# Full-width state sums and transpositions for the samples' heads

## The chip, the cores and the metric

The kernel runs on one core of one Trainium2 chip. The metric is the device time of one execution in microseconds (us); "the time before" is the median of three runs. The engines are TensorE (PE, with its weight loads shown apart as PEld), VectorE (DVE), ScalarE (ACT), GpSimd (POOL) and SyncE (SP), which issues most of the transfers.

## The reference

One layer of a hybrid decoder is computed for a prompt of 1024 tokens and for 8 samples of 4 tokens (32 rows, `NS`). A matrix-memory branch (mLSTM, 4 heads of 128 by 128) and a sliding-window attention run side by side on the same projected input; their outputs are gated, summed and projected. The change lies in the memory branch of the samples. There every sample brings its own state `C` per head, and the output of one head is

```
num = einsum('bhts,bhse->bhte', s, v) + w_inter * einsum('bhtd,bhde->bhte', q, C)
dot = sum(s) + w_inter * einsum('bhtd,bhd->bht', q, n)
h   = num / maximum(abs(dot), exp(-m_hat))
h   = h * rsqrt(mean(h * h) + NORM_EPS) * g_mn
```

All arithmetic is float32.

## The kernel before

The large products (input projections, output projections) are made on PE with operands split into a high and a low part, three products of 128x512 for each one of the reference; some are formed by a seven-product scheme for 2x2 blocks. This work is one long stream on PE, named `bx`, `bw`, `by`, `bz` in the middle of the kernel, `ax`, `aw`, `ay`, `az` for the attention's projection and `g_w_mo` and `foX`, `foW`, `foY`, `foZ` behind it. Its weights come by SP, ACT casts the high parts (`wh_...`) and DVE subtracts the low parts (`wl_...`).

Smaller pieces of work (attention units, memory heads, samples) are generators. A planner (`Side`) keeps an estimated clock, advanced by `mm` and `tr` with a cost per product, and lets a generator emit its next piece between two products of the stream when the delay that the generator yielded has passed and the PSUM banks that it named are free. The order of all PE instructions is fixed in the order in which they are emitted (`in_order`). In the middle of the kernel DVE and ACT are left to the framework, which orders by its own costs.

`sample_head(h)` is the generator of one head of the samples; it is run for h = 0 to 3, one at a time. Its first part makes the products of the 8 samples' queries with their states: 8 products `sn` with 32 stationary columns each, put in four strips of 32 PSUM partitions. So the 128 partitions of `ns4` (in the tile `sz`) hold four partial sums of the same 32 rows. Heads 0 and 2 only add theirs to the list `tails`. Heads 1 and 3 go on with a tail for two heads; here is what a *visit* means in this document:

- L1242 to L1246: the *state sums*. The four partial sums of a head are added on PE: the stationary operand is the piece of the constant table `cst` from column `C_S32` (745) with 32 columns, where row r has a one in column r mod 32; the moving operand is `ns4`, 128 by 129. Two such products, one for each head, go to the PSUM tile `st`, and ACT copies `st` to `sz` (32 partitions).
- L1247 to L1257: the squares, denominators and the scaling of both heads' rows, on ACT and DVE.
- L1258 to L1263: the *transpositions*. Each head's 32 by 128 rows are transposed on PE into the PSUM tile `sty`, and DVE scales each result by `gmn` into `gs`. In the code a transposition is followed by its scaling, then the second transposition and its scaling.

There are two such tails in the kernel, each with one visit for the state sums and one for the transpositions. `gs` is read some products later by the gate of the same head (`head_gate.samples`).

The column table continues behind `C_S32` (32 columns) with `C_BM` (8 columns, ones that tell which sample a row belongs to) and `C_S64` (64 columns, another summing pattern) and ends at `C_END` = 849: 104 columns in all.

In the profile every matmul has the line of the helper `mm` (L271), every transposition that of `tr` (L276) and the work of DVE and ACT in this part that of `call` (L220), so that groups are told apart by tile. A float32 matmul shows as two instructions of each kind, a transposition as one.

Of the kernel before, what the change touches and what calls it, by code (L numbers as in the profile page):

```python
# [15 lines left out]
ALU = mybir.AluOpType  # L16
# [8 lines left out]
NS = NB * NT  # L25
# [11 lines left out]
C_ID, C_S9, C_TRI, C_CM, C_AM, C_TS, C_CS, C_RS, C_S32, C_BM, C_S64 = 0, 128, 137, 265, 393, 649, 681, 713, 745, 777, 785  # L37
C_END = 849
# [135 lines left out]
def body(tc, a):  # L174
    nc = tc.nc
    with ExitStack() as ctx:
# [11 lines left out]
        def pb(shape, name):  # L188
            return ps.tile(shape, F32, tag="b", bufs=2, name=name)

        def po(shape, name):
            return ps.tile(shape, F32, tag="o", bufs=2, name=name)

        def ht(shape, name, dt=F32):
            return sp.tile(shape, dt, tag="half", bufs=50, name=name)

        def sm(shape, name, bufs=3, dt=F32):
            return sp.tile(shape, dt, tag=name, bufs=bufs, name=name)
# [8 lines left out]
        def in_order(ins, eng="PE"):  # L207
            i = getattr(ins, "ins", ins)
            no_sync(i, [last[eng]] if eng in last else [])
            last[eng] = i  # L210
# [27 lines left out]
        V, S, G = Ordered(nc.vector, "V"), Ordered(nc.scalar, "S"), Ordered(nc.gpsimd, "G")  # L238
# [28 lines left out]
        def mm(out, lhsT, rhs, start, stop, share=1, more=False):  # L267
            n = int(np.prod(rhs.shape[1:]))
            side.now += max(n, 250) / 2400 if rhs.dtype == F32R else max(n * 4 // share, 128) / 2400
            side.products += 1  # L270
            in_order(nc.tensor.matmul(out, lhsT, rhs, start=start, stop=stop, skip_group_check=more))  # L271

        def tr(out, in_, idn):
            side.now += 0.11
            side.products += 1
            in_order(nc.tensor.transpose(out, in_, idn))  # L276
# [43 lines left out]
        cst = cp.tile([128, C_END], F32, name="cst")  # L320
# [3 lines left out]
        ident = cst[:, C_ID:C_ID + 128]  # L324
# [4 lines left out]
        gmn, bada, gnorm = vec[:, 0:4], vec[:, 4:20], vec[:, 20:28]  # L329
# [656 lines left out]
        gs = cp.tile([128, NH, NS], F32, name="gs")  # L986
# [51 lines left out]
        def head(h):  # L1038
# [128 lines left out]
            if h == 2:  # L1167
                at["n0"], at["n1"] = (cp.tile([128, NH, NB], F32, name=n) for n in ("n0", "n1"))
                dma(at["n0"], a["state_n"])
                for i in range(NH):  # L1170
                    side.add("s", sample_head(i), "ob")
# [3 lines left out]
        def sample_head(h):  # L1175
            an, sxb, fls, wes = st["an"], st["sxb"], st["fls"], st["wes"]
            z = ht([128, 512], "sz")
# [28 lines left out]
            for b, m in zip(bs, ns_):  # L1206
                vf, vm = ht([NS, 512], f"vf{h}"), ht([96, 512], f"vm{h}", F32R)
                w = m * 129 + m % 2
# [31 lines left out]
                return  # L1240
            yield 3.0, "o"
            tot = po([128, 2, 129], f"st{h}")  # L1242
            for i, (_, n4) in enumerate(tails):
                mm(tot[:NS, i], cst[:, C_S32:C_S32 + NS], n4, start=True, stop=True)
            ns = z[:NS, 0:258].rearrange("p (m e) -> p m e", e=129)
            S.copy(ns, tot[:NS])  # L1246
            ssq = sm([NS, 2], "sssq", 2)  # L1247
            for i in range(2):
                jk = sm([128, 128], "mjk", 2, BF16)
# [6 lines left out]
            for i in range(2):  # L1256
                V.tensor_scalar(ns[:, i, 0:128], ns[:, i, 0:128], d[:, i:i + 1], r[:, i:i + 1], op0=ALU.mult, op1=ALU.mult)  # L1257
            yield 4.0, "b"  # L1258
            ty = pb([128, 2, NS], f"sty{h}")
            for i, (g, _) in enumerate(tails):  # L1260
                tr(ty[:, i], ns[:, i, 0:128], ident[:NS, :NS])
                V.tensor_scalar(gs[:, g], ty[:, i], gmn[:, g:g + 1], None, op0=ALU.mult)
                samples_done.append(g)  # L1263
            tails.clear()
            if h == NH - 1:
# [1108 lines left out]
```

## Time and profile before

| | |
|---|---|
| Median of three runs | 834.73 us (834.29 to 835.82) |
| Profiled execution, its own time | 832.12 us |
| Its span in the trace | 830.4 us |
| PE busy | 810.4 us (98%), 5129 instructions |
| PE weight loads busy | 669.3 us (81%) |
| DVE busy | 593.8 us (72%) |
| ACT busy | 420.5 us (51%) |
| POOL busy | 67.2 us (8%) |
| Granted PE clock, mean | 0.997 |

The profiled execution is 2.6 us shorter than the median of the runs, and 1.7 us longer than its own span. In the timelines each row has the start, the duration, the engine, the line, the operation, the tile written and the tiles read, and (for PE) the size of the stationary operand as rows*columns and of the result. Matmuls overlap: what a piece of work costs PE is read from the starts, not from the durations.

### The profile page before, as it was taken

To read this page: it belongs to the slowest core of one execution; us is meant where nothing else is said; L and a number is where in the kernel's file an instruction comes from. 1 tells how busy PE (TensorE), PEld (TensorE's weight loads), DVE (VectorE), ACT (ScalarE), POOL (GpSimd) and SP (SyncE) were. 2 spreads that over 40 slices of the span, in tenths; PEclk is the share of its full clock that TensorE was granted. 3 is DMA by queue.
4 is the path that set the end of the run, shared out by engine and by line. 5 is a ranking of instruction groups with operands and counts; after the bars stand their busy time and mean duration, and the time that the engine had idled before them with its cause. 6 is when DMAs were issued, how large, how long until landed. Compare 5 with 4: busy or idle time off the path is not lost. (4 is left out here: it accounts for less than half of the span.)

```text
span 830.4 us, 15038 instructions
## 1 busy us (share of the span) xinstructions
PE 810.4 (98%) x5129; PEld 669.3 (81%) x5129; DVE 593.8 (72%) x1479; ACT 420.5 (51%) x1030; POOL 67.2 (8%) x128
## 2 busy tenths in 40 slices
PE   6999999999999999999899999999999999999996
PEld 3779897888788788888788877887888789997775
DVE  4889886656656456475577785897569988974776
ACT  5664365555474564555455453544346654334343
POOL 0120000000000001000001000000002104250000
PEclk9999999999999999999999999999999999999998
DMA  9997766356436425479856345464336785643633
GB/s 334 378 357 238 184 201 213 118 150 217 143 111 189 114 85 150 140 240 286 268 188 205 120 141 155 143 203 142 103 117 196 230 288 172 212 146 122 202 109 108
DMA packets 106689, 153.96 MB, mean 185 GB/s; under 512 B 20448, under 2 KB 54368, under 8 KB 106580
## 3 DMA queue, kind: packets, MB, share of 16 engines
q1 hardware_dynamic: 100964, 142.25, 54.1%
q10 hardware_dynamic: 4176, 6.56, 2.2%
q0 software_dynamic: 1472, 4.20, 1.4%
q8 instruction: 40, 0.66, 0.3%
q14 instruction: 37, 0.30, 0.1%
HBM read 109.22 MB, written 44.75 MB: 185 GB/s over the span
## 5 line engine op out<-in xcount | busy, mean ns | idle before, releaser
L220 ACT ACTIVATE p<-p,nmx 128x256 f32<-128x256 f32 (+1 forms) x64 | 31.0, 486 | 12.4 <-DVE nmx L220 12.1
L271 PE MATMUL g_aq<-h_h,wh_aq 128*128 128x384 f32 (+1 forms) x96 | 32.2, 336 | 0.0
L271 PE MATMUL g_aq<-h_h,wl_aq 128*128 128x384 f32 (+1 forms) x96 | 30.9, 322 | 0.0
L271 PE MATMUL g_aq<-h_l,wh_aq 128*128 128x384 f32 (+1 forms) x96 | 30.8, 321 | 0.0
L271 PE MATMUL g_w_mo<-ym_l,wh_w_mo 128*128 128x384 f32 (+1 forms) x96 | 30.8, 321 | 0.0
L271 PE MATMUL g_w_mo<-ym_h,wh_w_mo 128*128 128x384 f32 (+1 forms) x96 | 30.8, 321 | 0.0
L271 PE MATMUL g_w_mo<-ym_l,wl_w_mo 128*128 128x384 f32 (+1 forms) x96 | 30.8, 321 | 0.0
L220 DVE CUSTOM_DVE_ANT_0 p<-sc,cst,sink 128x256 f32<-128x256 f32 (+1 forms) x64 | 26.2, 464 | 5.3 <-PE sc L271 5.2
L259 POOL DMA_DIRECT2D oD<-uqv x16 | 8.9, 554 | 183.2 <-ACT uqv L220 161.0
L220 DVE COPY p<-pt 128x512 f32<-128x512 f32 (+1 forms) x16 | 10.5, 657 | 13.6 <-PE pt L276 13.6
L271 PEld LDWEIGHTS g_aq<-h_h,wh_aq 128*128 128x128 f32 x96 | 18.0, 188 | 2.5 <-issue 1.5
L271 PEld LDWEIGHTS g_w_mo<-ym_l,wh_w_mo 128*128 128x128 f32 x96 | 18.0, 188 | 0.0
L271 PEld LDWEIGHTS g_aq<-h_l,wh_aq 128*128 128x128 f32 x96 | 18.1, 188 | 0.0
L271 PEld LDWEIGHTS g_w_mo<-ym_h,wh_w_mo 128*128 128x128 f32 x96 | 18.0, 188 | 0.0
L271 PE MATMUL sc<-ukv,uqv 64*128 64x256 f32 (+1 forms) x128 | 18.0, 390 | 0.0
L271 PEld LDWEIGHTS g_aq<-h_h,wl_aq 128*128 128x128 f32 x96 | 18.0, 188 | 0.0
L271 PEld LDWEIGHTS g_w_mo<-ym_l,wl_w_mo 128*128 128x128 f32 x96 | 18.0, 188 | 0.0
L220 ACT ACTIVATE p<-p,den 128x256 f32<-128x256 f32 (+1 forms) x32 | 14.5, 491 | 5.7 <-DVE den L220 5.6
L220 ACT ACTIVATE sq<-rows_h 128x512 f32<-128x512 f32 (+2 forms) x14 | 8.2, 582 | 17.8 <-issue 12.0
L220 DVE TENSOR_TENSOR et<-et,S 128x384 f32<-128x384 f32 (+1 forms) x12 | 6.1, 510 | 15.4 <-PE S L271 12.7
L271 PE MATMUL g_mq<-h_h,wh_mq 128*128 128x384 f32 (+1 forms) x48 | 16.8, 349 | 0.3 <-ACT mk L220 0.3
L276 PE MATMUL pt<-cst,p 128*128 128x128 f32 x120 | 16.4, 277 | 0.5 <-DVE mx L220 0.5
(2073 smaller groups left out, 2841.4 us busy)
## 6 DMA issues: line engine op xcount, KB each, us to landing
x<-xT SPq DMA_DIRECT2D x16, 256.0 KB, 5.6
early_h<-w_ada SPq DMA_DIRECT2D x8, 512.0 KB, 9.0
adar_ga<-w_ada SPq DMA_DIRECT2D x16, 256.0 KB, 4.0
wr_ga<-w SPq DMA_DIRECT2D x16, 256.0 KB, 2.9
wr_gm<-w SPq DMA_DIRECT2D x16, 256.0 KB, 3.6
taD<-gt SPq DMA_DIRECT2D x16, 256.0 KB, 2.2
tmD<-gt SPq DMA_DIRECT2D x16, 256.0 KB, 5.3
wor<-w_out SPq DMA_DIRECT2D x16, 256.0 KB, 5.1
```

The costliest lines, as they stand in the source:

```text
L220: ins = f(*args, **kw)
L259: ins = (eng or nc.sync).dma_start(out, in_)
L271: in_order(nc.tensor.matmul(out, lhsT, rhs, start=start, stop=stop, skip_group_check=more))
L276: in_order(nc.tensor.transpose(out, in_, idn))
```

## The change

The state sums take the stationary columns from `C_S32` to `C_END`, 104 instead of 32; their result has 104 partitions, of which the first 32 are the ones needed, and ACT's copy takes all 104. The two transpositions of a visit take all 104 partitions as input, with a 104 by 104 identity as moving operand, and their result has 128 by 104 elements for each head; the PSUM tile `sty` grows from 32 to 128 columns per head. The scaling of the squares, denominators and rows still works on the first 32 partitions. The two transpositions are emitted one behind the other, and then the two scalings, which read the first 32 columns.

```
             tot = po([128, 2, 129], f"st{h}")
+            w = C_END - C_S32
             for i, (_, n4) in enumerate(tails):
-                mm(tot[:NS, i], cst[:, C_S32:C_S32 + NS], n4, start=True, stop=True)
-            ns = z[:NS, 0:258].rearrange("p (m e) -> p m e", e=129)
-            S.copy(ns, tot[:NS])
+                mm(tot[:w, i], cst[:, C_S32:C_END], n4, start=True, stop=True)
+            nw = z[:, 0:258].rearrange("p (m e) -> p m e", e=129)
+            S.copy(nw[:w], tot[:w])
+            ns = nw[:NS]
...
             yield 4.0, "b"
-            ty = pb([128, 2, NS], f"sty{h}")
+            ty = pb([128, 2, 128], f"sty{h}")
+            for i in range(2):
+                tr(ty[:, i, 0:w], nw[:w, i, 0:128], ident[:w, :w])
             for i, (g, _) in enumerate(tails):
-                tr(ty[:, i], ns[:, i, 0:128], ident[:NS, :NS])
-                V.tensor_scalar(gs[:, g], ty[:, i], gmn[:, g:g + 1], None, op0=ALU.mult)
+                V.tensor_scalar(gs[:, g], ty[:, i, 0:NS], gmn[:, g:g + 1], None, op0=ALU.mult)
                 samples_done.append(g)
```

PE at the first state sums: the rows are products of the stream (`bw`, 128x512, from a block and a split weight), and between them the two sums.

```order
 L271 MATMUL bw<-t2l_1093,wh_pgate_6__5970 128x512
 L271 MATMUL bw<-t2h_1092,wl_pgate_6__5971 128x512
-L271 MATMUL st_6039<-sz,cst 32x129 x2
+L271 MATMUL st_6039<-sz,cst 104x129 x2
 L271 MATMUL bw<-t2h_1370,wh_pgate_6__5970 128x512
 L271 MATMUL bw<-t2l_1371,wh_pgate_6__5970 128x512
```

Their place stays; only the width of the result differs. It is the same at the second state sums (`st_6738`).

PE at the second pair of transpositions, with the semaphores for which each instruction waits (`DVE_49` counts DVE's finished instructions):

```order
 L271 MATMUL by<-t3l_1686,wh_phead_gate_7__6815 128x512
 L271 MATMUL by<-t3h_1685,wl_phead_gate_7__6816 128x512
-L276 MATMUL sty_6908<-cst,sz 128x32 [waits DVE_49] x2
+L276 MATMUL sty_6908<-cst,sz 128x104 [waits DVE_49]
+L276 MATMUL sty_6908<-cst,sz 128x104
 L271 MATMUL bx<-h_h_378,wh_phead_gate_1__6838 128x512
 L271 MATMUL bx<-h_l_379,wh_phead_gate_1__6838 128x512
```

The place is the same again. The second transposition waited for the first scaling on DVE, which reads the same PSUM tile; it now waits for nothing of its own. At the first pair (`sty_6175`) the second transposition still names DVE, but there the count is that of its own input, the rows in `sz` scaled before, and no longer that of a scaling to `gs`.

DVE at the same visit (`hg1z` and `hg` belong to the gates of a head, `wl_...` and `ws` to the weights of coming products):

```order
 L220 TENSOR_TENSOR hg1z<-p_6811,by 128x512
-L220 TENSOR_SCALAR gs<-sty_6908,vec 128x32
+L220 TENSOR_SCALAR gs<-sty_6908,vec 128x32 x2
 L220 TENSOR_TENSOR wl_phead_gate_5__6931<-ws_6883,wh_phead_gate_5__6930 128x512
 L220 TENSOR_SCALAR hg_6903<-hg_6903,hg1z 128x512
-L220 TENSOR_SCALAR gs<-sty_6908,vec 128x32
 L220 TENSOR_TENSOR ws_7072<-wr_mz_0_6979,wr_mz_1_6981 128x512
```

The second scaling moves ahead of the low part of a weight and of a gate product. Nothing else moves on any engine, SP's and POOL's queues included.

## The prediction

> **What bounds the kernel now.** First the page's busy times, then the busy time by stretches: PE is the engine to look at.
>
> ```profile
> PE 810.4 (98%) x5129; PEld 669.3 (81%) x5129; DVE 593.8 (72%) x1479; ACT 420.5 (51%) x1030; POOL 67.2 (8%) x128
> ```
>
> ```profile
> 580.00:640.00 60.00, 59.67 (x319) 49.23 (x320) 42.01 (x72) 28.16 (x54) 4.11 (x3) 1.00 0.41 122
> ...
> 760.00:800.00 40.00, 40.00 (x186) 30.32 (x185) 25.01 (x56) 17.97 (x46) 0.00 (x0) 1.00 0.36 125
> 800.00:830.40 30.40, 23.21 (x126) 19.99 (x124) 22.70 (x54) 11.14 (x32) 0.00 (x0) 0.92 0.41 143
> ```
>
> The columns are the stretch, its length, and the busy times of PE, PEld, DVE, ACT and POOL, the granted clock, the share of the DMA engines and their GB/s. PE has no idle time from 680 us to 800, and the idle time behind it is the tail after its last product. So a microsecond taken out of PE's stream ahead of that is a microsecond of the end, unless something else turns out late. Third, the list of PE's own waits from 500 us on, with the sum, the count and the longest:
>
> ```profile
> PE sty L276 <- DVE gs L220: 1.1, 2, 0.8
> PE aw L271 <- ACT aw L220: 0.2, 1, 0.2
> ```
>
> These two are all of it. The first is in the changed lines: the second transposition waits for the scaling of the first. But a busy PE need not be a PE that streams, so the fourth view is PE's timeline at the four visits, read by starts.
>
> **The state sums.** The first visit in full, and of the second the product ahead of it and the second product behind it:
>
> ```profile
> 503.05 0.39 PE L271 MATMUL bw<-t2h,wl_pgate__5971 128*128 128x512 f32 x1
> 503.37 0.63 PE L271 MATMUL st<-sz,cst 128*32 128x129 f32 x4
> 503.93 0.50 PE L271 MATMUL bw<-t2h,wh_pgate__5970 128*128 128x512 f32 x1
> 504.26 0.39 PE L271 MATMUL bw<-t2l,wh_pgate__5970 128*128 128x512 f32 x1
> ...
> 563.88 0.39 PE L271 MATMUL by<-t4h,wl_pquery_gate__6676 128*128 128x512 f32 x1
> ...
> 565.09 0.39 PE L271 MATMUL by<-t4l,wh_pquery_gate__6675 128*128 128x512 f32 x1
> ```
>
> I measure each piece from the start of the last stream product ahead of it to the start of the second one behind it, since the first one behind starts slowly (0.33 us to the next). That is 504.26 - 503.05 = 1.21 us, and 565.09 - 563.88 = 1.21. No row has 104 stationary columns. The nearest above is two float32 products of 129 columns with all 128 stationary columns, `U` of a prompt's head, also inside the stream:
>
> ```profile
> 341.80 0.39 PE L271 MATMUL bx<-h_h,wl_pgate__4064 128*128 128x512 f32 x1
> 342.03 0.61 PE L271 MATMUL U<-hv,hk 128*128 128x129 f32 x4
> 342.39 0.48 PE L271 MATMUL bw<-h_h,wh_pgate__4138 128*128 128x512 f32 x1
> 342.71 0.40 PE L271 MATMUL bw<-h_l,wh_pgate__4138 128*128 128x512 f32 x1
> ```
>
> The same four instructions cost 342.71 - 341.80 = 0.91 us. They start 0.23 us behind the product ahead, where `st` needs 0.32, and take 0.36 against 0.56. The weight loads tell why:
>
> ```profile
> 503.37 0.36 PEld L271 LDWEIGHTS st<-sz,cst 128*32 128x32 f32 x4 [0.35 <-issue]
> ```
>
> ```profile
> 341.81 0.64 PEld L271 LDWEIGHTS U<-hv,hk 128*128 128x128 f32 x4
> ```
>
> The loads of `U` begin under the stream's last product (341.80); those of `st`, with 32 columns, start only at 503.37, after 0.35 us of idle time. So a narrow stationary operand is not loaded ahead, and its width is not what it costs. I take the full-width price: 104 columns fill more than three quarters of the array, and a narrow one of three quarters in the other direction exists, `sU` with 96 rows:
>
> ```profile
> 472.80 0.40 PE L271 MATMUL by<-t4h,wl_pgate__5616 128*128 128x512 f32 x1
> 473.03 0.64 PE L271 MATMUL sU<-vm,skn 96*128 96x388 f32 x3
> 473.51 0.40 PE L271 MATMUL by<-t4h,wh_pgate__5615 128*128 128x512 f32 x1
> ```
>
> It starts 0.23 us behind the product ahead: no delay. So a visit falls from 1.21 to 0.91, 0.30 us, and two visits give **0.60 us**. The ends are no gain at all (104 treated like 32) and the strips among the rivals below.
>
> [...]
>
> ACT's copy of the sums reads 104 partitions for 32, with the same 258 elements in each:
>
> ```profile
> L220 ACT COPY sz<-st x2: 361/362/364, 504.0 to 565.4; 32x258 f32<-32x258 f32 x2
> ```
>
> ```profile
> L220 ACT COPY uqv<-oT x16: 352/373/378, 117.3 to 320.5; 128x256 f32<-128x256 f32 x16
> ```
>
> 128 partitions take 373 ns at the median where 32 take 362, so I cost it at 0.01 us twice, off PE's path, and at nothing.
>
> **The transpositions.** First visit in full; of the second the product ahead, the second transposition and the second product behind:
>
> ```profile
> 516.14 0.39 PE L271 MATMUL bw<-h_h,wl_pgate__6128 128*128 128x512 f32 x1
> 516.46 0.24 PE L276 MATMUL sty<-cst,sz 32*128 32x32 f32 x1
> 517.04 0.24 PE L276 MATMUL sty<-cst,sz 32*128 32x32 f32 x1 [0.35 <-DVE gs L220]
> 517.22 0.50 PE L271 MATMUL bw<-h_h,wh_pgate__6127 128*128 128x512 f32 x1
> 517.55 0.39 PE L271 MATMUL bw<-h_l,wh_pgate__6127 128*128 128x512 f32 x1
> ```
>
> ```profile
> 579.00 0.39 PE L271 MATMUL by<-t3h,wl_phead_gate__6816 128*128 128x512 f32 x1
> ...
> 580.33 0.24 PE L276 MATMUL sty<-cst,sz 32*128 32x32 f32 x1 [0.77 <-DVE gs L220]
> ...
> 580.85 0.40 PE L271 MATMUL bx<-h_l,wh_phead_gate__6838 128*128 128x512 f32 x1
> ```
>
> They cost 517.55 - 516.14 = 1.41 us and 580.85 - 579.00 = 1.85. For full-height transpositions in the stream there are eight of a prompt's head, `ty`:
>
> ```profile
> 444.02 0.39 PE L271 MATMUL bw<-h_h,wl_pgate__5275 128*128 128x512 f32 x1
> 444.25 1.03 PE L276 MATMUL ty<-cst,et 128*128 128x128 f32 x8
> 445.05 0.48 PE L271 MATMUL bw<-h_h,wh_pgate__5274 128*128 128x512 f32 x1
> 445.36 0.40 PE L271 MATMUL bw<-h_l,wh_pgate__5274 128*128 128x512 f32 x1
> ```
>
> Eight take 1.34 us by the same measure, 0.80 of it the eight, 0.10 each. With six fewer that is 1.34 - 0.60 = 0.74 us for two, as wide as 128 columns; 104 are no wider. The wait is gone too: nothing stands between the two transpositions, and the second one's own input was scaled before the visit. So the visits fall by 1.41 - 0.74 = 0.67 and 1.85 - 0.74 = 1.11, together **1.78 us**.
>
> What is moved on DVE: the second scaling now goes ahead of a weight's low part.
>
> ```profile
> 580.03 0.25 DVE L220 TENSOR_SCALAR gs<-sty,vec 128x32 f32<-128x32 f32 x1
> 580.19 0.68 DVE L220 TENSOR_TENSOR wl_phead_gate__6931<-ws,wh_phead_gate__6930 128x512 fp32r<-128x512 f32 x1
> ```
>
> ```profile
> 589.30 0.39 PE L271 MATMUL bz<-h_h,wl_phead_gate__6931 128*128 128x512 f32 x1
> ```
>
> That delays this low part by the 0.16 us of one scaling (580.19 - 580.03), and PE needs it nine microseconds later, so it costs nothing; if the slack were gone, 0.16. Later products that now name DVE's semaphore do so for things that the removed wait had covered; those are as old as before. DVE also waited for the second transposition behind the first scaling; that ends, and no waiting instruction stands behind it.
>
> **The sum.** 0.60 + 1.78 = 2.38 us. The profiled execution took 832.12, and would take 829.74. It lies 2.61 below the median of the runs, 834.73; the pieces are steps of PE's stream and do not depend on that difference, so against the median it is 834.73 - 2.38 = 832.35, forecast as **832.4 us**, 0.28% less. A change of 0.2%, 1.67 us, is about what a measurement of this kernel can tell from no change.
>
> **The rivals.**
>
> *The narrow treatment stays, only the wait goes.* If 104 columns or rows were loaded late as 32 are, the starts would stay slow, and only the steps between the two transpositions would shrink: from 517.04 - 516.46 = 0.58 to the 0.18 that an unhindered one takes (517.22 - 517.04), and by the second wait's row from 1.01 to 0.18, if the first of that pair stands 0.32 behind 579.00 as in the first pair. That is 0.40 + 0.83 = 1.23 us, a time of 833.5. For it: no row has 104 columns. Against it: `sU` with 96 rows is not delayed.
>
> *The gain is eaten before the attention's projection.* PE's other wait, 0.2 us at `aw`, ends a chain that runs through DVE:
>
> ```profile
> 646.46 1.11 DVE yr L220
> ```
>
> ```profile
> 627.24 0.69 DVE L220 TENSOR_TENSOR hg<-p,bw 128x512 f32<-128x512 f32 x1 [0.28 <-PE bw L271]
> ```
>
> If DVE did not get there sooner, PE would come 2.38 us earlier and wait for just as much: 834.7. For it: DVE was nearly the bound there. Against it: the work that it does then was itself released by PE's product at 627.24, so it moves along with PE.
>
> *The array takes 104 as four strips of 32.* This one makes it slower. The inner part of the state sums, 0.56 us, would then be paid four times, 3 x 0.56 x 2 visits = 3.36 us more, and each transposition four times its 0.18, 3 x 0.18 x 4 = 2.16 more, less the 1.23 of the wait: 4.29 more, 839.0. It decides from the point where the strips cost over 1.23 + 1.67 = 2.90 us. Against it: three strips of rows in `sU` run at the stream's pace, 0.16 us for a product of 388 columns (0.48 for three).
>
> **How the numbers follow.** Full gain 0.74, narrow treatment stays 0.10, eaten 0.09, strips 0.07. The best case is the full gain without the slow first product behind each piece, which `U` still shows (0.32 against 0.23): four times 0.09, so 2.74 and 832.0. The runs spread 1.5 us; half of it, 0.77, is added on both sides. Low is 832.0 - 0.77, 831.2; high is the narrow case plus as much, 833.5 + 0.77, 834.3. These hold 0.84 of the cases. Faster by over 0.2%: 0.70, the full gain less a few hundredths for the runs' scatter; within 0.2%: 0.22; slower by over 0.2%: 0.08.
>
> **What would show it.** Right: the loads of `st` begin under the product ahead, `st` starts 0.23 us behind it, and the piece measures about 0.91; the two transpositions stand 0.1 us apart, without a wait on DVE, the piece about 0.74; PE's wait at `aw` stays at some tenths, and its last product ends 2.4 us earlier. Wrong: an idle time of 0.35 ahead of the loads as before (narrow treatment), a wait of over 2 us between 640 and 650 (eaten), or pieces longer than 1.21 (strips). Transfers that land at other times, from 640 us on, could move the end without any of this.

## The result and the profile after

The changed kernel takes 831.21 us (median of five runs, 830.73 to 832.2) where the one before takes 834.73 (832.91 to 835.82 with the runs made beside it). The ratio is 0.997, with a 95% interval of 0.9955 to 0.9984: faster by 1.3 to 3.8 us. Its profiled execution took 830.97 us, with a span of 829.2. The forecast was 832.4, and the measured time lies at the lower edge of its range, so two questions remain: whether the parts do what the prediction says, and where another microsecond came from.

The page's busy times of the changed kernel, and PE's own waits from 490 us on (sum, count, longest):

```profile
PE 810.1 (98%) x5129; PEld 670.8 (81%) x5129; DVE 592.7 (71%) x1479; ACT 420.6 (51%) x1030; POOL 67.5 (8%) x128
```

```profile
PE aw L271 <- ACT aw L220: 0.2, 1, 0.2
```

The wait at `sty`, 1.1 us in two, is gone. The one at `aw` is as long as it was. PE's timeline of the changed kernel at the state sums, the first visit in full and of the second the product ahead and the second behind:

```profile
504.46 0.39 PE L271 MATMUL bw<-t2h,wl_pgate__5971 128*128 128x512 f32 x1
504.69 0.60 PE L271 MATMUL st<-sz,cst 128*104 128x129 f32 x4
505.04 0.47 PE L271 MATMUL bw<-t2h,wh_pgate__5970 128*128 128x512 f32 x1
505.36 0.39 PE L271 MATMUL bw<-t2l,wh_pgate__5970 128*128 128x512 f32 x1
...
564.22 0.39 PE L271 MATMUL by<-t4h,wl_pquery_gate__6676 128*128 128x512 f32 x1
...
565.12 0.39 PE L271 MATMUL by<-t4l,wh_pquery_gate__6675 128*128 128x512 f32 x1
```

The weight loads at the first of them:

```profile
504.46 0.61 PEld L271 LDWEIGHTS st<-sz,cst 128*104 128x104 f32 x4
```

The loads now begin at 504.46, together with the stream's last product ahead, and no idle time stands before them. `st` starts 0.23 us behind that product, and the piece is 505.36 - 504.46 = 0.90 us where it was 1.21; the second is 0.90 too. The transpositions of the changed kernel, first visit in full, of the second three rows:

```profile
517.23 0.39 PE L271 MATMUL bw<-h_h,wl_pgate__6128 128*128 128x512 f32 x1
517.46 0.34 PE L276 MATMUL sty<-cst,sz 104*128 104x104 f32 x2
517.58 0.47 PE L271 MATMUL bw<-h_h,wh_pgate__6127 128*128 128x512 f32 x1
517.89 0.39 PE L271 MATMUL bw<-h_l,wh_pgate__6127 128*128 128x512 f32 x1
...
579.02 0.39 PE L271 MATMUL by<-t3h,wl_phead_gate__6816 128*128 128x512 f32 x1
579.26 0.34 PE L276 MATMUL sty<-cst,sz 104*128 104x104 f32 x2
...
579.69 0.39 PE L271 MATMUL bx<-h_l,wh_phead_gate__6838 128*128 128x512 f32 x1
```

The two stand in one row, with no wait: 517.89 - 517.23 = 0.66 us and 579.69 - 579.02 = 0.67, where the pieces were 1.41 and 1.85. Together the four visits give 0.31 + 0.31 + 0.75 + 1.18 = 2.55 us. With PE's products of the two traces laid side by side, the changed kernel is 1.41 us late ahead of the first visit (504.46 against 503.05) and 1.16 early behind the fourth (579.69 against 580.85): 2.57 us. PE's last product, in the kernel before and then in the changed one, is 1.19 us early, so all of it reaches the end:

```profile
822.93 0.28 PE L271 MATMUL foY<-wo_p0h,u3wlD 128*128 128x256 f32 x1
```

```profile
821.74 0.28 PE L271 MATMUL foY<-wo_p0h,u3wlD 128*128 128x256 f32 x1
```

What made it late ahead of the first visit lies at 404 us, far from the change. The kernel before in two stretches of 4 us (length, busy times of PE, PEld, DVE, ACT and POOL, then the granted clock):

```profile
404.00:408.00 4.00, 1.67 (x12) 1.35 (x12) 1.65 (x4) 1.99 (x9) 0.10 (x1) 1.00 0.86 320
408.00:412.00 4.00, 4.00 (x44) 3.40 (x46) 2.46 (x5) 2.94 (x8) 0.00 (x0) 1.00 0.70 233
```

The changed kernel in the same two stretches, and what PE does there:

```profile
404.00:408.00 4.00, 1.74 (x10) 1.50 (x9) 1.38 (x3) 1.73 (x8) 0.10 (x1) 0.86 0.78 296
408.00:412.00 4.00, 4.00 (x15) 3.17 (x14) 2.32 (x4) 2.22 (x5) 0.00 (x0) 0.72 0.57 210
```

```profile
406.80 1.21 PE L271 MATMUL S<-hq,hk 128*128 128x128 f32 x4 [2.26 <-DVE C L220]
...
408.66 0.63 PE L271 MATMUL bw<-t2h,wl_pgate__4793 128*128 128x512 f32 x1
409.08 0.63 PE L271 MATMUL bx<-h_h,wh_pgate__4824 128*128 128x512 f32 x1
```

PE waits 2.26 us for DVE (2.33 in the kernel before), and then its products follow each other in 0.42 us instead of 0.23, at a granted clock of 0.72 in the mean of the stretch. In the profiled execution of the kernel before the same wait was followed by steps of 0.23 us, at a clock of 1.00. Whether such a half-speed stretch belongs to the change or to the single execution, these two profiles can't tell; the profiles of the experiments tell more of it.

### The profile page after: what moved, and what is told of

Its sections match the earlier page's. It is cut to its first block, busy times and chain, and to the rows that moved or that the text cites. A ratio compares the mean times of both kernels' runs of the same rounds, so it can differ in the third digit from the quotient of the medians.

```text
span 829.2 us, 15039 instructions
## 1 busy us (share of the span) xinstructions
PE 810.1 (98%) x5129; PEld 670.8 (81%) x5129; DVE 592.7 (71%) x1479; ACT 420.6 (51%) x1030; POOL 67.5 (8%) x128
```

## The experiments

Pieces are measured throughout as in the prediction: from the start of the last product of the stream ahead to the start of the second one behind. The theory to be tested: the width pays only where it lets the stationary operand be loaded ahead, the emitted order pays by taking PE's wait for the first scaling away, and the two add up at the end. The rivals: the gain comes from elsewhere (other executions of one of the two kernels are disturbed more), the width acts by degrees and not by a threshold, or the wait at `sty` is not due to the shared PSUM tile. Edits are shown against the changed kernel. In the table the changed kernel has five runs, each of the three parts twelve, and the kernel before 29 beside them (five beside the first row of the changed kernel).

| kernel | state sums, us | transpositions, us | median (lowest to highest), us | before, beside it | ratio, 95% interval |
|---|---|---|---|---|---|
| before | 1.21, 1.21 | 1.41, 1.85 | 834.73 | | |
| changed | 0.90, 0.90 | 0.66, 0.67 | 831.21 (830.73 to 832.2) | 834.73 | 0.9955 to 0.9984 |
| changed, again | 0.89, 0.89 | 0.67, 0.67 | 830.19 (829.96 to 831.71) | 834.29 | 0.9943 to 0.9966 |
| sums wide only | 0.89, 0.90 | 1.42, 1.84 | 833.75 (831.56 to 836.2) | 834.29 | 0.9979 to 1.0007 |
| order only | 1.22, 1.21 | 0.89, 0.89 | 832.76 (830.79 to 835.63) | 834.29 | 0.9965 to 0.9991 |
| width only | 0.90, 0.90 | 1.23, 1.73 | 833.64 (831.17 to 836.6) | 834.29 | 0.9979 to 1.0007 |

**The changed kernel again**, without an edit.

> The changed kernel once more, beside the three halves of the change on the same chip. Theory (PE's stream lost 2.57 us at the four visits and all of it reaches the end): the pieces, from the start of the last product ahead to the start of the second behind, measure 0.90, 0.90, 0.66 and 0.67 us, and the ratio to the kernel before is 0.997. Rival (part of the 3.5 us between the first medians was the change acting elsewhere): the offset of PE's products to those of the kernel before moves at other places too, at the same ones each time; the half-speed stretch of PE at 407 to 410 us, seen in the first profile of the changed kernel, comes back.

The pieces came out as expected; the time is 4.1 us less than that of the kernel before on the same chip, more than the 2.55 of the pieces. So the excess is not confined to one comparison. This profile has the half-speed stretch too: a wait of 3.2 us at `S`, and a granted clock of 0.57 from 408 to 412.

**The sums wide, the transpositions as before.**

```
             ty = pb([128, 2, 128], f"sty{h}")
-            for i in range(2):
-                tr(ty[:, i, 0:w], nw[:w, i, 0:128], ident[:w, :w])
             for i, (g, _) in enumerate(tails):
+                tr(ty[:, i, 0:NS], ns[:, i, 0:128], ident[:NS, :NS])
                 V.tensor_scalar(gs[:, g], ty[:, i, 0:NS], gmn[:, g:g + 1], None, op0=ALU.mult)
```

> Only the state sums have 104 columns; the transpositions take 32 rows and follow each other in the old order. Theory: sums 0.90 us each instead of 1.21, transpositions 1.41 and 1.85 as before, 0.62 us less in all, ratio 0.9993. Rival (the width helps only where the neighbour is wide too): sums still 1.21, ratio 1.000.

0.32 and 0.31 us by the pieces, 0.5 by the medians, and the interval holds no change. The sums alone are below what the runs can tell.

**The order alone**, with 32 columns and rows.

```
-            w = C_END - C_S32
+            w = NS
...
-                mm(tot[:w, i], cst[:, C_S32:C_END], n4, start=True, stop=True)
+                mm(tot[:w, i], cst[:, C_S32:C_S32 + w], n4, start=True, stop=True)
...
-                tr(ty[:, i, 0:w], nw[:w, i, 0:128], ident[:w, :w])
+                tr(ty[:, i, 0:NS], ns[:, i, 0:128], ident[:NS, :NS])
```

> Only the order: both transpositions ahead of both scalings, 32 columns and 32 rows as before. Theory: the wait for DVE goes (0.40 and 0.84 us), the late start and the slow first product behind stay, so the transposition pieces measure about 1.0 us each (0.32 + 0.18 + 0.18 + 0.33), sums 1.21; 1.24 us less, ratio 0.9985. Rival (the order alone does nearly everything): pieces near 0.7, ratio 0.998 or less.

PE's timeline of this kernel at the first visit:

```profile
516.32 0.39 PE L271 MATMUL bw<-h_h,wl_pgate__6128 128*128 128x512 f32 x1
516.64 0.30 PE L276 MATMUL sty<-cst,sz 32*128 32x32 f32 x2
516.87 0.50 PE L271 MATMUL bw<-h_h,wh_pgate__6127 128*128 128x512 f32 x1
517.21 0.39 PE L271 MATMUL bw<-h_l,wh_pgate__6127 128*128 128x512 f32 x1
```

0.89 us, 0.11 less than expected: the two together take 0.23 (516.87 - 516.64), where 0.18 for each was expected. The late start of 0.32 stays. The order is worth 0.52 + 0.96 = 1.48 us, the largest part of the change; by the medians it is 1.5.

**The width alone**, with a transposition followed by its scaling as before.

```
             ty = pb([128, 2, 128], f"sty{h}")
-            for i in range(2):
-                tr(ty[:, i, 0:w], nw[:w, i, 0:128], ident[:w, :w])
             for i, (g, _) in enumerate(tails):
+                tr(ty[:, i, 0:w], nw[:w, i, 0:128], ident[:w, :w])
                 V.tensor_scalar(gs[:, g], ty[:, i, 0:NS], gmn[:, g:g + 1], None, op0=ALU.mult)
```

> Only the width: sums with 104 columns, transpositions with 104 rows, but each transposition followed by its scaling. Theory: sums 0.90 each; the second transposition still waits for the first scaling, so the pieces measure about 1.25 and 1.75 us (0.1 to 0.2 less than before each); 0.9 us less in all, ratio 0.9989. Rival (the wait was only a matter of the narrow form): no wait, pieces near 0.67, ratio 0.997.

The second visit of this kernel:

```profile
580.61 0.39 PE L271 MATMUL by<-t3h,wl_phead_gate__6816 128*128 128x512 f32 x1
580.84 0.25 PE L276 MATMUL sty<-cst,sz 104*128 104x104 f32 x1
581.94 0.31 PE L276 MATMUL sty<-cst,sz 104*128 104x104 f32 x1 [0.85 <-DVE gs L220]
```

The first starts 0.23 us behind the product ahead, on time, and then the second waits 0.85 for DVE. An earlier start of the first mostly lengthens the wait: at this visit only 0.12 us of the width's 0.22 remain. So the two edits of the transpositions are worth more together (0.22 each by the width, once the wait is gone) than the width is alone.

**Other widths.** In one kernel the sums and transpositions of the first tail have 64 columns and rows and those of the second 72, in another 40 and 96.

```
-            w = C_END - C_S32
+            w = 64 if h == 1 else 72
...
-                mm(tot[:w, i], cst[:, C_S32:C_END], n4, start=True, stop=True)
+                mm(tot[:w, i], cst[:, C_S32:C_S32 + w], n4, start=True, stop=True)
```

> The changed kernel with other widths: 64 columns and rows in the tail of head 1, 72 in that of head 3. Theory (a stationary operand is loaded ahead only if it is over half of the array in both directions): head 1 as narrow as with 32, sums 1.21 us and transpositions about 1.0; head 3 as with 104, sums 0.90 and transpositions 0.66. Rival (the price falls with the width, step by step or in proportion): 64 lies between, sums near 1.1, and 72 is not yet at 0.90.

> The same with 40 in the tail of head 1 and 96 in that of head 3. Theory (over half): 40 is narrow, sums 1.21 and transpositions about 1.0; 96 is wide, 0.90 and 0.66. Rival (only full strips of 32 count, or 104 is special): 96 is narrow, or 40 costs more than 32 did because it takes two strips.

The state sums of the first of these kernels, with 64 and then with 72 stationary columns:

```profile
507.09 0.39 PE L271 MATMUL bw<-t2h,wl_pgate__5971 128*128 128x512 f32 x1
507.41 0.65 PE L271 MATMUL st<-sz,cst 128*64 128x129 f32 x4
...
508.33 0.40 PE L271 MATMUL bw<-t2l,wh_pgate__5970 128*128 128x512 f32 x1
...
567.45 0.39 PE L271 MATMUL by<-t4h,wl_pquery_gate__6676 128*128 128x512 f32 x1
567.68 0.60 PE L271 MATMUL st<-sz,cst 128*72 128x129 f32 x4
...
568.36 0.39 PE L271 MATMUL by<-t4l,wh_pquery_gate__6675 128*128 128x512 f32 x1
```

| width | state sums, us | transpositions, us |
|---|---|---|
| 40 | 1.22 | 0.90 |
| 64 | 1.24 | 0.92 |
| 72 | 0.91 | 0.64 |
| 96 | 0.91 | 0.66 |
| 104 | 0.90 | 0.66 |

Single executions took 834.18 us (64 and 72) and 834.0 (40 and 96), beside 835.92 for the kernel before; the pieces tell more. It is a threshold between 64 and 72 of 128, in columns (the sums) and in rows (the transpositions) alike, and not a price that falls with the width: 40 columns cost as much as 64, 72 as much as 104. At 64 and below the first instruction starts 0.32 us behind the stream, above it 0.23. Other small products of the kernel before show the same border. `sc` with 64 rows is late:

```profile
216.18 0.39 PE L271 MATMUL bx<-h_h,wl_phead_in__2696 128*128 128x512 f32 x1
216.50 1.14 PE L271 MATMUL sc<-ukv,uqv 64*128 64x256 f32 x8
```

All five `sc` with 64 rows and all seven `oT` with 64 columns that stand right behind a 128x512 product of the stream start 0.32 to 0.33 us behind it, and the four `sU` with 96 rows 0.23 to 0.24. What the delay is made of is not shown by any run here. What is measured is 0.09 us of late start, 0.02 on the way back (0.33 to 0.34 to the second product behind, 0.31 to 0.32 above the border), and for the four instructions of the sums another 0.2 us inside the piece.

**Two PSUM tiles.** The order of the kernel before and 32 columns, but the second transposition goes to a tile of its own.

```
-            for i in range(2):
-                tr(ty[:, i, 0:w], nw[:w, i, 0:128], ident[:w, :w])
             for i, (g, _) in enumerate(tails):
-                V.tensor_scalar(gs[:, g], ty[:, i, 0:NS], gmn[:, g:g + 1], None, op0=ALU.mult)
+                t = ty if i == 0 else pb([128, 2, 128], f"stz{h}")
+                tr(t[:, i, 0:NS], ns[:, i, 0:128], ident[:NS, :NS])
+                V.tensor_scalar(gs[:, g], t[:, i, 0:NS], gmn[:, g:g + 1], None, op0=ALU.mult)
```

The sums have 32 columns too (`w = NS`, as in the kernel with the order alone).

> The kernel before but for one thing: the second transposition of a visit writes a PSUM tile of its own instead of the other half of the first one's, with the old widths and the old order in the code. Theory (the wait comes from the shared tile, not from the order of the instructions on PE): the wait for DVE is gone although the code's order is the old one, transposition pieces about 1.0 us each, sums 1.21. Rival (PE's order of emission makes the wait): the waits of 0.35 and 0.77 us stay, pieces 1.41 and 1.85. A third possibility: the second tile's bank is not free yet, and the second transposition waits for ACT instead.

```profile
518.24 0.39 PE L271 MATMUL bw<-h_h,wl_pgate__6128 128*128 128x512 f32 x1
518.56 0.24 PE L276 MATMUL sty<-cst,sz 32*128 32x32 f32 x1
518.64 0.22 PE L276 MATMUL stz<-cst,sz 32*128 32x32 f32 x1
518.79 0.50 PE L271 MATMUL bw<-h_h,wh_pgate__6127 128*128 128x512 f32 x1
```

PE's timeline of this kernel, above, shows the second transposition 0.08 us behind the first, without a wait, and the pieces are 0.89 and 0.89 as with the order alone (a single execution took 832.73 us). So it takes both, the shared tile and the read between the two writes, to make the wait: here the order in the code is the old one, with the order alone the tile is still shared, and in both the wait is gone.

**The same at another place.** Four times in this part a head's scores `sS` are made with 32 stationary columns behind two transpositions `stk`. Here `sS` takes the keys of all heads, 128 columns, of which DVE reads the head's 32 rows.

```
-            mm(S_[:NS], ks[:, h], qs[:, h], start=True, stop=True)
+            mm(S_, ks.rearrange("p h s -> p (h s)"), qs[:, h], start=True, stop=True)
...
-            V.tensor_tensor(et, et, S_[:NS], op=ALU.mult)
+            V.tensor_tensor(et, S_[h * NS:h * NS + NS], et, op=ALU.mult)
```

> The changed kernel, and the product of keys and queries of each samples' head takes the keys of all four heads as stationary operand (128 columns instead of 32); DVE reads the 32 partitions of its head. Theory: the product is no longer late behind the two transpositions ahead of it; the piece from the start of the last stream product ahead to the start of the second behind falls from 1.05 us to about 0.95 at each of four heads, 0.4 us in all, too little to be told in the time. Rival: the transpositions with 32 columns ahead of it take the delay over, and the piece stays at 1.05.

PE's timeline of the changed kernel, and then of this one, from the second transposition on:

```profile
454.36 0.27 PE L276 MATMUL stk<-cst,vs 128*32 128x128 f32 x1
454.56 0.25 PE L271 MATMUL sS<-qs,ks 128*32 128x32 f32 x2
454.74 0.50 PE L271 MATMUL bz<-h_h,wh_pgate__5315 128*128 128x512 f32 x1
```

```profile
455.02 0.27 PE L276 MATMUL stk<-cst,vs 128*32 128x128 f32 x1
455.13 0.31 PE L271 MATMUL sS<-qs,ks 128*128 128x32 f32 x2
455.27 0.48 PE L271 MATMUL bz<-h_h,wh_pgate__5315 128*128 128x512 f32 x1
```

`sS` starts 0.11 us behind the transposition instead of 0.20, and passes in 0.14 instead of 0.18. The pieces are 0.90, 0.91, 0.91 and 0.90 where they were 1.05, so it gives 0.6 us in all, 0.2 more than expected. A single execution took 831.13 us. So a narrow matmul starts 0.09 us late at a third place too; inside the piece the price is smaller than at the sums, 0.04 instead of 0.2.

**The wait at 404 us taken away.** All ten profiles so far have a wait of PE of 1.9 to 3.4 us at `S`, and eight of them a half-speed stretch behind it (all but the kernel before and the one with the order alone): products that follow each other in 0.42 to 0.43 us instead of 0.23, and a granted clock of 0.50 to 0.72 from 408 to 412 us. Laid beside the kernel before, these eight lose between 1.5 us (changed kernel) and 4.0 (widths 40 and 96) from the product ahead of the wait to 416 us, part of it by a longer wait. What PE waits for is DVE's third step of a chain `C`. DVE in the changed kernel:

```profile
404.54 0.56 DVE L220 TENSOR_TENSOR et<-et,cst 128x384 f32<-128x384 f32 x1 [2.07 <-DMA et<-nmd]
405.92 0.56 DVE L220 TENSOR_TENSOR qw<-qw,hq 128x384 f32<-128x384 f32 x1 [0.83 <-DMA qw<-wid]
406.40 0.34 DVE L220 SCALAR_TENSOR_TENSOR C<-C,dec,U 128x129 f32<-128x129 f32 x1
```

The step stands behind two preparations that wait for transfers. In the next kernels they are ordered behind the chain's last step; nothing else in DVE's order moves, and it changes at this one place.

```
+                for i in (i1, i2):
+                    no_sync(getattr(i, "ins", i), chain_op)
...
                     chain.append(Cn)
+                chain_op[:] = [getattr(ci, "ins", ci)]
```

(`i1` and `i2` are the preparations `et` and `qw` in `prep`, `ci` the step of the chain in `stage_b`.) First with the wide scores in it, then without:

> The changed kernel with two more edits: the scores of the samples take all 128 stationary columns (as in the run with wide scores, measured 0.05 to 0.15 us at each of four places), and on DVE the third step of the chain C stands ahead of the two preparations et and qw that wait for transfers. In the changed kernel's profile PE waits 2.26 us at 404.5 to 406.8 for that step, which stood behind qw; DVE had been idle since 402.5, so the step can end near 402.9, and PE's wait should be gone (below 0.3 us; et and qw are read by PE only at 421.7). Theory A, the half-speed stretch of PE behind 407 us comes from that wait: with it gone the granted clock is 1.00 in 404 to 412, steps of the stream are 0.23 throughout, and the median is about 831.2 - 0.6 - 2.3 = 828.3, or up to 2 us less where the stretch is in most executions of the changed kernel; the runs scatter less. Theory B, the stretch has another cause: the wait goes, but steps of 0.43 still show there. Rival: the wait is given back at a later point, since the products ahead then meet weights that land late; the time is as that of the changed kernel, and PE waits at a weight between 407 and 480.

> The changed kernel with DVE's third step of the chain C ahead of et and qw alone, the scores narrow as before. Against the run with both edits it should be about 0.6 us slower (what the wide scores gave by their pieces), and against the changed kernel 2.3 us faster by the wait alone, and up to 2 more by the half-speed stretch if theory A holds (granted clock 1.00 in 404 to 412 in this profile too). If the rival holds, about the time of the changed kernel, 830 to 831.

The second of the two, DVE and the two stretches:

```profile
403.38 0.35 DVE L220 SCALAR_TENSOR_TENSOR C<-C,dec,U 128x129 f32<-128x129 f32 x1 [0.78 <-PE n L271]
405.03 0.56 DVE L220 TENSOR_TENSOR et<-et,cst 128x384 f32<-128x384 f32 x1 [1.29 <-DMA et<-nmd]
406.85 0.56 DVE L220 TENSOR_TENSOR qw<-qw,hq 128x384 f32<-128x384 f32 x1 [1.26 <-DMA wr_ga<-w]
```

```profile
404.00:408.00 4.00, 4.00 (x25) 3.45 (x24) 1.71 (x4) 3.69 (x13) 0.10 (x1) 1.00 0.92 323
408.00:412.00 4.00, 4.00 (x47) 3.27 (x46) 3.44 (x6) 1.30 (x4) 0.00 (x0) 1.00 0.83 269
```

PE is busy throughout, at a granted clock of 1.00. This kernel takes 827.13 us (826.85 to 828.48; ratio to the kernel before 0.9915, 0.99 to 0.9929), and with the wide scores 826.32 (825.97 to 827.06; 0.9902, 0.9888 to 0.9916), 0.8 us less. Both are faster than the changed kernel, and theory A holds as far as these runs go: where the wait is gone, so is the stretch, in both profiles (with the wide scores the products of the stream step by 0.23 us from 405 to 408). The rival did not come true: PE waits at no weight between 407 and 480 us in either.

**The change without the disturbance.** The same edit of DVE's order in the kernel before, and the changed kernel with it once more on the same chip.

> The kernel before, with nothing of the change, but with DVE's third step of the chain C ahead of et and qw. PE's wait of about 2 us at 404 and the half-speed stretch that varies with the execution should be gone (granted clock 1.00 in 404 to 412), so that it can be compared with the changed kernel in the same form without them. If the change itself is worth what its pieces measure, this kernel is 2.57 us slower than that one: 827.1 + 2.6 = 829.7, and its pieces are 1.21, 1.21, 1.41, 1.85 again. If the difference of the first medians, 3.5 us, is the change's own, it is 830.6 or more.

> The changed kernel with the chain ahead once more, on the same chip as the one above, for the difference of the two: 827.1, 2.6 us below it if the pieces are the whole of the change, 3.5 or more if they are not. Pieces 0.90, 0.90, 0.66, 0.67.

The first of these two in the second stretch:

```profile
408.00:412.00 4.00, 4.00 (x47) 3.27 (x46) 3.36 (x6) 1.77 (x4) 0.00 (x0) 1.00 0.80 261
```

It takes 829.46 us (829.23 to 829.95), the changed one in the same form 827.02 (826.91 to 827.46), and their spans are 828.2 and 825.7. Its pieces are 1.21, 1.22, 1.42 and 1.84, those of the other 0.89, 0.89, 0.67 and 0.67: a sum of 2.57, and a difference of the medians of 2.44. The runs of this pair scatter over 0.7 and 0.6 us (those of the two kernels above over 1.6 and 1.1), where 29 runs of the kernel before, beside the first experiments, reached from 831.91 to 837.66. Beside this pair the kernel before took 832.7 us in nine runs, and 834.82 in the nine beside the two kernels above, on the same chip: its own median moved by 2.1 us without any edit.

## Why the prediction was right, and where a term was off

**What bounds the kernel.** That a microsecond out of PE's stream is a microsecond of the end held: 2.55 us by the pieces, 2.60 by the starts of PE's last product, 2.44 by the medians of the undisturbed pair.

**The state sums.** "So a visit falls from 1.21 to 0.91" was right to 0.01 us (0.90), and for the reason given: the loads begin under the product ahead. Forecast 0.60, measured 0.62. A load of `st` takes 168 ns at the median instead of 110, 58 more, but the longer loads lie beside the products: the first begins 0.23 us ahead of `st` (504.46 against 504.69).

**The transpositions.** Right in mechanism (the wait goes, and the late start goes), and off in size: the mis-sized step is "With six fewer that is 1.34 - 0.60 = 0.74 us for two". It took two transpositions at 0.10 us each, from `ty`; two of 104 columns pass in 0.12 (517.58 - 517.46), and the pieces are 0.66 and 0.67. So the term is 0.75 + 1.18 = 1.93 where 1.78 was forecast. That 104 columns are fewer than 128 is the smaller part of it: a pair passes in 0.10 us with 72, 0.11 with 96 and 0.12 with 104, and by that trend in 0.13 to 0.14 with 128 (an estimate), where the prediction had 0.20. So the price of one `ty` in a run of eight did not carry over to a pair; why was not tried. The experiments divide the gain as order 1.48, width of the transpositions 0.44 on top of it, width of the sums 0.62.

**What lies beside.** ACT's copy of 104 partitions takes 372 ns at the median instead of 362, as costed. The later low part of a weight on DVE made PE wait nowhere.

**The rivals.** "The narrow treatment stays" would have been right with 64 columns or fewer, as the runs with 40 and 64 show, and not with 104. The prediction weighed it with `sU` alone; the `sc` and `oT` of the same trace, with 64 rows and columns, would have shown from below where the border can lie. Its price was for the wait alone 1.23 us; the wait alone was worth 1.48, since the two narrow transpositions pass in 0.23 together and not in 0.18 each. "Eaten before the attention's projection" is excluded by the wait at `aw`, still 0.2 us. Strips of 32 would have made the pieces longer, and they are shorter than before, 0.66 to 0.90 us.

**The time.** The step from the sum to the time failed by more than the sum did: "the pieces are steps of PE's stream and do not depend on that difference, so against the median it is 834.73 - 2.38 = 832.35". The pieces don't, but the two medians do, since the profiled executions lose a varying time at and behind the wait at 404 us (1.5 to 4.0 us more than the kernel before, in eight of ten), and with that wait gone the runs scatter less (by 0.6 to 1.6 us). The prediction looked at the waits from 500 us on, where the change lies, and not at this one. Of the 3.5 us between the medians some 2.5 are the change, as the undisturbed pair shows, and about 1 is left, which the two sets of runs would then have lost differently. Such a rest needs no reason of its own: the median of the kernel before moved by 2.1 us between two sets on one chip. Whether the changed kernel is also disturbed less for a reason stays open. Both comparisons gave more than the pieces (3.5 and 4.1 us), which speaks for it. The two profiles say little: the profiled execution of the kernel before has no half-speed stretch and lies 2.6 us below the median of its runs, so it is not a typical one. That the measured time lies at the lower bound of the range, 831.2, and not near 834.73 - 2.55 = 832.18 is owed to this rest, and not to a mechanism that was forecast.

## What to carry to other kernels

Where a small float32 matmul stands inside a stream of full ones, widen its stationary operand, in rows and in columns, if there are columns at hand that do no harm (72 of 128 were enough here, 64 were not): the only other cost seen here was 0.01 us in each of ACT's copies, and it took 0.31 us from each pair of sums. Emit all PE writes to a PSUM tile ahead of the first read of it, or give each its own tile; a read in between made PE wait 0.35 to 0.85 us. And look through the whole list of waits for one that could set off a slow stretch (here waits of 1.9 to 3.4 us were followed by one in eight of ten profiles), even far from the change, before the medians of two kernels are compared to a quarter of a percent.

## What the runs showed of the hardware

**Half speed behind a wait.** Ten profiles have a PE wait of 1.9 to 3.4 us, and in eight of them the products behind it step by 0.42 to 0.43 us instead of 0.23. In the two with the longest of these stretches (widths 64 and 72, 40 and 96) the granted clock from 408 to 412 us is 0.50. If it is 0.50 in all eight, the clocks of the three stretches from 404 to 416 us give the length, 3.4 us in six of them and 6.8 in two (an estimate): in the changed kernel (0.14 + 0.28) x 4 us / 0.5 = 3.4. In three of the four profiles without the wait the clock was 1.00 from 404 to 416 us; in the fourth, with the wide scores, the products of the stream step by 0.23 us. The length of the wait does not decide alone: 2.33 us in the kernel before were followed by a clock of 1.00, 2.26 in the changed one by 0.72. What decides, and what sets the length of a stretch, no run here shows.

**A narrow transposition that is not late.** The `stk` transpositions, with 32 stationary columns and 128 rows, start 0.23 us behind the stream as a wide one does, while the matmul with 32 columns behind them is 0.09 late. Transpositions with 64 rows or fewer are late (0.32). Matmuls are late with few columns (`st`, 0.32 with 32; `oT`, 0.32 with 64) and with few rows (`sc`, 0.32 with 64). So with 32 columns and 128 rows it is the operation that makes the difference in these rows, and for transpositions only the number of rows counted; why was not tried.
